# A two-layer decoder trunk: layer 0's raw weights on GpSimd's queue, transposing transfers one half product earlier, products with values and joins one later

## The chip, the cores and the metric

The kernel runs on one core of a Trainium2 chip. The metric is the device time of one execution in microseconds (us); lower is better. Five engines work side by side, each through its own instructions in order: TensorE (PE: matrix products, PEld: its weight loads), VectorE (DVE), ScalarE (ACT), GpSimd (POOL) and SyncE (SP), which here only issues transfers (DMAs). An instruction that waits holds up everything behind it on its engine. A transfer that an engine has issued is carried out by the core's 16 DMA engines, and a semaphore tells when it has landed.

## What is computed

A causal decoder trunk of two layers on 1024 rows of width 1024, all in float32. Layer 0 mixes tokens by dilated attention in three groups (g = 0, 1, 2) of eight heads of width 128, layer 1 by gated linear attention, and each is followed by a dense squared-ReLU network. Cut to the part that matters here:

```python
def dilated_attention(h, w_in, w_out):
    qkv = (h @ w_in).reshape(B, S, N_GROUPS, 3, ATTN_HEADS, HEAD_DIM)
    for g, (window, dil) in enumerate(((128, 1), (512, 4), (2048, 16))):
        q = apply_rope(qkv[:, :, g, 0], cos, sin) * HEAD_DIM ** -0.5
        k = apply_rope(qkv[:, :, g, 1], cos, sin)
        v = qkv[:, :, g, 2]
        o_g, lse_g = dilated_group_attention(q, k, v, dil, window // dil)
    alpha = softmax(stack(lses), axis=0)           # the three groups are merged
    o = sum(alpha[..., None] * stack(outs), axis=0)
    return o.reshape(B, S, ATTN_WIDTH) @ w_out
```

## The kernel before

Layer 0 has three stages. First come the values of all groups (the class `Values`), then the queries and keys of the 24 pairs of a head and a group with their attention (the class `Heads`), then the output product (`out_proj`). The change lies in the second stage, from 246 us to about 870 us of the span.

**A pair** p = 3h + g is worked off in `run_head` (L1182). The queries and keys of a pair come from seven products (slots) of 12 matrix instructions in float32r halves, and each slot is cut into two half products of six. After each of the 14 half products `advance` moves a clock by one and runs what an agenda holds for that tick, in the order of a rank. So the agenda, written by hand, sets the order of all engines' instructions: what is put at tick c + 14 comes in program order behind 14 half products of the pair that began at tick c = 14p. The pairs overlap: while the products of pair p run, the attention of pair p - 1 (`follow`) is put between them, and its last products fall into pair p + 1.

**The raw weights.** `Heads.load` (L1113) loads the weights of the next pair at tick c + 3 by four transfers of 256 KB (L1119) into two tiles named raw. ScalarE and VectorE cut them into halves (wah, wal and so on, L536 and L537) from tick c + 8 on, and the products of the next pair read these from tick c + 14 on.

**The columns.** `column` (L1122) adds up a quarter of queries or keys (c, L1127), and SP swaps the halves of its partitions for the rotary positions by two transfers (cw, L1128 and L1129). Four ticks later VectorE multiplies with cosines and sines and writes qT or kT (L1136 to L1144). The columns come at ticks 5, 11, 13 and 15.

**The attention of a pair** goes over four blocks j of 256 queries. `scores` multiplies queries and keys on TensorE (pS, L989); `soft` does the mask and the exponentials (pt, L1003 and L1005); `halves` (L1027) splits the 32-bit words into 16-bit parts on ScalarE (L1035), and GpSimd's queue writes them to DRAM (pscr, L1037); `flip` (L1040) reads them back by a transposing transfer on SP's queue (L1048); and `values` (L1059) multiplies with the values (pO, L1069), copies the result (orow, L1073) and stores it (og, L1076 to L1082). The table `POINTS` (L1191) has one row each for the ticks of scores, halves, flips and values, in that order, with one number for each j; `load_values` stands two ticks before the first scores. `SINGLE` is the table of the last two attentions, which transpose on TensorE instead. A flip waits for the write of its part to land. In group 1, and for j = 0 of group 0, a block needs two writes and two flips, else one.

**The joins.** When all three groups of a head are stored, `plan_merges` (L1300) puts the merge on the agenda: it loads half of the rows (rows, L1207, 780 KB), weighs and scales them, and joins them (om, L1231 and L1232). The halves are loaded at ticks 13 and 24 of the head's successor.

**The end of the stage.** In the last pair, the first four tiles of the output weights (`W.dma`, L136, 512 KB each) and the first half of the joined heads 0 to 3 (`ahead_h8`, name ol, L1292, 1 MB) are loaded at ticks 1 to 3, and `turned.turn(0)` transposes ol on TensorE (L260) at tick 8.

Of the kernel before, what the change touches and what calls it, by code (L numbers as in the profile page):

```python
# [20 lines left out]
P = 128  # L21
# [21 lines left out]
def hybrid_trunk(ctx, tc, x, norm_mix, norm_mlp, norm_fin, a_in, a_out, g_in, g_up, g_b, g_nw,  # L43
                 g_out, m_up, m_down, tab, msk, gmask, ident_d, out):
    nc = tc.nc
    pe, act, dve, pool, sp = nc.tensor, nc.scalar, nc.vector, nc.gpsimd, nc.sync
# [7 lines left out]
    def h8(shape, dt, name):  # L54
        return wk.tile(shape, dt, name=name, tag="h8", bufs=12)

    def k4(shape, dt, name):
        return wk.tile(shape, dt, name=name, tag="k4", bufs=25)
# [53 lines left out]
    class Weights:  # L112
# [14 lines left out]
            self.slots.append(src)  # L127
            self.by.append(by)

        def dma(self):  # L130
            n = self.ndma
            if n < len(self.slots):
                self.ndma += 1
                src = self.slots[n]
                self.raws[n] = k4([P] + list(src.shape[1:]), F32, "raw")
                sp.dma_start(self.raws[n], src)  # L136

        def prep(self, eng=dve):
            n = self.nprep
# [41 lines left out]
    W = Weights()  # L181
# [8 lines left out]
    def add_rows(w, k0, by=None):  # L190
        for k in range(2):
            W.add(w[P * (k0 + k):P * (k0 + k + 1), :], by and by(k0 + k))
# [93 lines left out]
    class Split:  # L286
# [4 lines left out]
        @staticmethod  # L291
        def at(tiles, k):
            n = 4 // len(tiles)
            return tiles[k // n][:, k % n, :]
# [206 lines left out]
    class Up:  # L501
# [10 lines left out]
        def load(self, p):  # L512
            if p < NP:
                self.raw[p] = [k4([P, 4, 256], F32, "raw") for _ in range(2)]
                for k in range(2):
                    sp.dma_start(self.raw[p][k], cols(self.w, 256 * p, 256, 4 * k, 4))
# [220 lines left out]
    oscr = drp.tile([S, D], F32, name="oscr")  # L737
# [363 lines left out]
    class Heads(Up):  # L1101
# [11 lines left out]
        def load(self, p):  # L1113
            if p < self.count:
                h, g = divmod(p, NG)
                self.raw[p] = [k4([P, 4, 256], F32, "raw") for _ in range(2)]
                for k in range(2):
                    for b in range(2):
                        sp.dma_start(self.raw[p][k][:, :, 128 * b:128 * b + 128],  # L1119
                                     self.w[:, 4 * k:4 * k + 4, 3 * g + b, HD * h:HD * h + HD])  # L1120

        def column(self, p, b, half, bank_, e):  # L1122
# [59 lines left out]
        def run_head(self, p):  # L1182
            self.plan(p)
            if p:
                self.follow(p - 1, 14 * p, self.POINTS if p < self.count - 1 else self.SINGLE)
            for s in self.SLOTS:
# [1 line left out]
                    self.product(p, s, range(2 * half, 2 * half + 2))  # L1188
                    advance()

        POINTS = (8, 8, 12, 12), (11, 12, 15, 16), (20, 20, 24, 24), (14, 15, 18, 19)  # L1191
        SINGLE = (8, 10, 12, 14), (12, 14, 16, 18), (14, 16, 18, 20)

        def follow(self, p, c, points):
# [8 lines left out]
    def merge_load(h, half):  # L1203

        rows = (h8([P, 4, NG, HD + 2], F32, "rows") if h == HEADS - 1 and half else
                r6([P, 4, NG, HD + 2], "rows"))
        sp.dma_start(rows, og[h][512 * half:512 * half + 512].rearrange("(t p) g c -> p t g c", p=P))  # L1207
        return rows

    def merge_weights(rows):  # L1210
        d = sm([P, 4, NG], "md")
        e = sm([P, 4, NG], "me")
        z = sm([P, 4], "mz")
        dve.tensor_reduce(z, rows[:, :, :, HD + 1], axis=AX.X, op=OP.min)
        dve.tensor_tensor(d, z.unsqueeze(2).to_broadcast([P, 4, NG]), rows[:, :, :, HD + 1], op=OP.subtract)
        act.activation(e, d, AF.Exp)
        return d, e, z

    def merge_shares(rows, d, e, z):
        dve.tensor_tensor(d, e, rows[:, :, :, HD], op=OP.mult)  # L1220
        dve.tensor_reduce(z, d, axis=AX.X, op=OP.add)
        dve.reciprocal(z, z)
        dve.tensor_tensor(e, e, z.unsqueeze(2).to_broadcast([P, 4, NG]), op=OP.mult)

    def merge_scale(rows, e, t):
        for g in range(NG):
            act.activation(rows[:, t, g, 0:HD], rows[:, t, g, 0:HD], AF.Copy, scale=e[:, t, g:g + 1])

    def merge_join(rows, eng):
        o = t2([P, 4, HD], F32, "om")  # L1230
        eng.tensor_tensor(o, rows[:, :, 0, 0:HD], rows[:, :, 1, 0:HD], op=OP.add)  # L1231
        eng.tensor_tensor(o, o, rows[:, :, 2, 0:HD], op=OP.add)  # L1232
        return o
# [8 lines left out]
    def merges(h, done):  # L1242

        rows, part = {}, {}

        def load(half):
            rows[half] = merge_load(h, half)

        def start(half):
            part[half] = merge_weights(rows[half])  # L1250

        def finish(half):
            done(h, half, merge(rows.pop(half), *part.pop(half)))
        return load, start, finish
# [25 lines left out]
    def merged(h, half, o):  # L1280
        if h < HEADS - 1:
            sp.dma_start(oscr[512 * half:512 * half + 512, HD * h:HD * h + HD].rearrange("(b p) c -> p b c", p=P), o)
        else:
            def last():
                t_head(h, half, o)
                reached.add((0, half))
            at(clock[0] + 7, last)

    def ahead_h8(pairs):

        t = h8([P, 4, 512], F32, "ol")
        sp.dma_start(t, oscr[512 * pairs:512 * pairs + 512, 0:512].rearrange("(b p) c -> p b c", p=P))  # L1292
        return [t[:, 0:2, :], t[:, 2:4, :]]

    def ahead_k4(p):
# [4 lines left out]
    def plan_merges(h, c):  # L1300

        rows, part = {}, {}

        def load(half):
            rows[half] = merge_load(h, half)

        def weigh(half):
            part[half] = merge_weights(rows[half])

        def join(half):  # L1310
            del part[half]
            merged(h, half, merge_join(rows.pop(half), dve))
        for half in range(2):
            t = c + 13 + 11 * half
            at(t, lambda half=half: load(half))
            if half and h == HEADS - 2:
                t += 9
            at(t + 4, lambda half=half: weigh(half), 9)
            at(t + 5, lambda half=half: merge_shares(rows[half], *part[half]), 9)
            for n in range(4):  # L1320
                at(t + 6 + n, lambda half=half, n=n: merge_scale(rows[half], part[half][1], n), 9)
            at(t + 10, lambda half=half: join(half), 9)
# [429 lines left out]
    ol = []  # L1752
    turned = Turned(ol, x[0])
    for p in range(heads.count):
        h, g = divmod(p, NG)
        if g == 1 and h:
            plan_merges(h - 1, 14 * p)
        if p == heads.count - 1:
            for k in range(0, KT, 2):
                add_rows(a_out, k)  # L1760
            c = 14 * p
            at(c + 1, lambda: (W.dma(), W.dma()), 0)
            at(c + 2, lambda: (W.dma(), W.dma()), 0)
            at(c + 3, lambda: ol.extend(ahead_h8(0)), 0)
            for t in (5, 6, 7, 8):
                at(c + t, lambda: W.prep(dve), 7)
            at(c + 8, lambda: turned.turn(0), 7)
            at(c + 9, lambda: (turned.load_x(0), turned.load_x(1)))
            at(c + 11, lambda: turned.turn(1), 7)
            at(c + 17, lambda: ol.extend(ahead_h8(1)), 9)  # L1770
        heads.run_head(p)
# [7 lines left out]
    def tail():  # L1779

        c = clock[0]
        heads.follow(heads.count - 1, c, ((6, 7, 8, 9), (9, 10, 11, 12), (11, 12, 13, 14)))
        load, start, finish = merges(HEADS - 1, merged)
        rows = {}
        advance()

        def early(half):
            t = rows[half] = h8([P, 4, 512], F32, "ol2")
            sp.dma_start(t[:, :, 0:384], oscr[512 * half:512 * half + 512, 512:896].rearrange("(b p) c -> p b c", p=P))
        at(c + 7, lambda: early(0))  # L1790
        at(c + 16, lambda: early(1))
        for i, (half, h) in enumerate(((0, 4), (0, 5), (0, 6), (1, 4), (1, 5), (1, 6))):
            at(c + (13 + 3 * i if half == 0 else 21 + i), lambda half=half, h=h: t_head(h, half, rows[half][:, :, HD * (h - 4):HD * (h - 4) + HD]))
        at(c + 15, lambda: (load(0), load(1)), 9)
        at(c + 18, lambda: start(0))
        at(c + 19, lambda: finish(0))
        at(c + 20, lambda: start(1))
        at(c + 21, lambda: finish(1))
        steps.extend([advance] * 42)
# [591 lines left out]
    ol, turn1 = [], []  # L2391
# [81 lines left out]
```

## Time and profile before

| | before |
|---|---|
| median of 3 runs | 2609.16 us (2606.06 to 2611.59) |
| the profiled execution | 2608.73 us |
| its span | 2607.0 us |
| TensorE busy | 2569.7 us (99%) |
| VectorE busy | 1865.2 us (72%) |
| ScalarE busy | 1309.1 us (50%) |
| GpSimd busy | 79.3 us (3%) |
| SP's queue of transfers | 437.29 MB, 55.3% of 16 engines' span |
| GpSimd's queue of transfers | 17.05 MB, 2.1% |

The span is what the trace covers; the execution takes 1.7 us more around it. A row of a list of waits reads: who waited, for whom, us in total, how often, the longest. A row of the timeline reads: start, us, engine, line, operation, out<-in, how many, and in brackets the idle time before it and what ended it. SPq is SP's issue of a transfer; the time beside it is that of the issue, not of the transfer. A row of one line's instructions has the shortest, median and longest duration in ns, and where it issues transfers a row has the same from issue to landing. A row of windows has, for each engine, the busy time and the number of instructions, then the granted TensorE clock, the busy share of the DMA engines and what they moved.

### The profile page before, as it was taken

What the parts mean: (1) busy time and instruction counts of PE and PEld (TensorE: products, weight loads), DVE (VectorE), ACT (ScalarE), POOL (GpSimd) and SP (SyncE); (2) the same over time, 40 slices, a digit from 0 to 9 for tenths busy, and PEclk for the clock granted to TensorE, in tenths of its full rate; (3) what the DMA queues carried; (4) which work ended last, traced back from release to release, by engine and by line L of the source; (5) the groups of instructions that cost most, each with busy time, mean ns of one, the idle gap of its engine ahead of it and who ended that gap; (6) DMA issues with size and microseconds to landing.
All of it is one profiled execution on the core that took longest, in us unless ns stands there. A gap on an engine that the chain in (4) does not pass through costs nothing.

```text
span 2607.0 us, 33382 instructions
## 1 busy us (share of the span) xinstructions
PE 2569.7 (99%) x11901; PEld 2138.2 (82%) x11901; DVE 1865.2 (72%) x3018; ACT 1309.1 (50%) x2388; POOL 79.3 (3%) x132
## 2 busy tenths in 40 slices
PE   9999999999998999999999999999999999999998
PEld 7888888888787888888888888888888888888887
DVE  7745888888887668766657487887658866656567
ACT  6423566666665446555534345654426555553334
POOL 0000111111110000000000000000000000000000
PEclk9999999999999999999999999999999999999999
DMA  5543688788888732544775453463513544396543
GB/s 182 172 143 109 171 210 213 203 208 216 207 212 219 238 121 100 191 153 154 257 268 185 145 184 106 124 213 99 183 67 127 170 150 161 126 354 205 182 149 131
DMA packets 403705, 456.73 MB, mean 175 GB/s; under 512 B 92337, under 2 KB 264753, under 8 KB 403538
## 3 DMA queue, kind: packets, MB, share of 16 engines
q1 hardware_dynamic: 397250, 437.29, 55.3%
q0 software_dynamic: 6144, 17.05, 2.1%
q8 instruction: 93, 1.52, 0.2%
q14 instruction: 74, 0.61, 0.1%
q10 hardware_dynamic: 144, 0.26, 0.0%
HBM read 279.19 MB, written 133.10 MB: 158 GB/s over the span
## 4 chain that ended last, share of the span: by engine, by line
PE 87%; DMA 5%; DVE 4%; ACT 2%; SPq 1%; issue 1%; DVEq 0%; ACTq 0%
PE pX L599 15%; PE pB L1936 13%; PE pA L1936 10%; PE pV L599 9%; PE pB L830 8%; PE pA L830 5%; PE pY L599 5%; PE pZ L599 5%; PE pd L216 3%; PE pd L214 3%; PE pd L215 3%; DMA cw<-c 2%; DMA pt<-pscr 1%; PE pS L989 1%; PE pO L1069 1%
## 5 line engine op out<-in xcount | busy, mean ns | idle before, releaser
L1936 PE MATMUL pB<-dh 128*128 128x512 f32 x512 | 199.4, 389 | 0.0
L1936 PE MATMUL pB<-dh,dl 128*128 128x512 f32 x512 | 199.2, 389 | 0.0
L1936 PE MATMUL pB<-dl,dh 128*128 128x512 f32 x512 | 199.2, 389 | 0.0
L223 DVE TENSOR_TENSOR dl<-sin,dh 128x1024 fp32r<-128x1024 f32 x112 | 136.7, 1220 | 42.1 <-ACT dh L220 41.4
L220 ACT ACTIVATE dh<-sin 128x1024 fp32r<-128x1024 f32 x112 | 117.9, 1052 | 88.6 <-PE pB L1936 34.1
L220 ACT ACTIVATE dh<-kept 128x1024 fp32r<-128x1024 f32 x64 | 67.9, 1061 | 183.4 <-DVE kept L1901 138.1
L599 PE MATMUL pV<-s4h,wd 128*128 128x512 f32 x448 | 150.9, 399 | 0.0
L1936 PE MATMUL pA<-dh 128*128 128x512 f32 x384 | 149.4, 389 | 0.0
L1936 PE MATMUL pA<-dl,dh 128*128 128x512 f32 x384 | 149.4, 389 | 0.0
L1936 PE MATMUL pA<-dh,dl 128*128 128x512 f32 x384 | 149.4, 389 | 0.0
L1005 ACT ACTIVATE pt<-pt,orow 128x128 f32<-128x128 f32 (+1 forms) x192 | 84.7, 442 | 123.7 <-DVE orow L1003 122.5
L1936 PEld LDWEIGHTS pB<-dh 128*128 128x128 f32 x512 | 96.1, 188 | 20.0
L1936 PEld LDWEIGHTS pB<-dh,dl 128*128 128x128 f32 x512 | 96.1, 188 | 19.9
L1936 PEld LDWEIGHTS pB<-dl,dh 128*128 128x128 f32 x512 | 96.1, 188 | 19.9
L537 DVE TENSOR_TENSOR wal<-raw,wah 128x512 fp32r<-128x512 f32 x112 | 76.2, 686 | 41.1 <-ACT wah L536 41.1
L1069 PE MATMUL pO<-v,pt 128*128 128x128 f32 x560 | 79.2, 284 | 23.1 <-DMA pt<-pscr 22.7
L537 DVE TENSOR_TENSOR wbl<-t,wbh 128x1024 fp32r<-128x1024 f32 x56 | 68.6, 1225 | 46.3 <-ACT wbh L536 46.2
L608 ACT ACTIVATE c<-c 128x512 f32<-128x512 f32 x64 | 40.4, 631 | 118.6 <-DVE c L636 77.6
L1037 POOL DMA_DIRECT2D pscr<-pt x124 | 77.0, 621 | 752.3 <-ACT pt L1035 742.0
L1069 PEld LDWEIGHTS pO<-v,pt 128*128 128x128 f32 x560 | 73.5, 195 | 31.3 <-DMA pt<-pscr 27.7
L599 PEld LDWEIGHTS pV<-s4h,wd 128*128 128x128 f32 x448 | 84.2, 188 | 17.8 <-DVE rb L624 0.3
L223 DVE TENSOR_TENSOR dl<-kept,dh 128x1024 fp32r<-128x1024 f32 x64 | 78.4, 1225 | 24.7 <-ACT dh L220 18.7
(398 smaller groups left out, 7444.3 us busy)
## 6 DMA issues: line engine op xcount, KB each, us to landing
sin<-acts SPq DMA_DIRECT2D x112, 512.0 KB, 3.9
raw<-in_mlp_w_up_dram SPq DMA_DIRECT2D x64, 512.0 KB, 6.2
acts<-s SPq DMA_DIRECT2D x64, 512.0 KB, 3.3
raw<-in_mlp_w_down_dram SPq DMA_DIRECT2D x64, 512.0 KB, 4.7
raw<-in_attn_w_in_dram SPq DMA_DIRECT2D x98, 256.0 KB, 4.5
cw<-c SPq DMA_DIRECT2D x192, 128.0 KB, 3.2
acts<-c SPq DMA_DIRECT2D x64, 256.0 KB, 2.1
kept<-in_mlp_w_down_dram SPq DMA_DIRECT2D x32, 512.0 KB, 5.2
```

Of the source, the lines that this page charges most:

```text
L214: pe.matmul(ps, sh, mh, start=start, stop=False)
L215: pe.matmul(ps, sh, ml, start=False, stop=False)
L216: pe.matmul(ps, sl, mh, start=False, stop=stop)
L220: act.activation(hi, src, AF.Copy)
L223: dve.tensor_tensor(lo, src, hi.bitcast(F32), op=OP.subtract)
L537: self.remain(lambda: dve.tensor_tensor(lo, src, hi.bitcast(F32), op=OP.subtract))
L599: pe.matmul(st[b], u[:, k, :], v, start=first and k + n == 0, stop=k == 3 and n == 2, skip_group_check=True)
L830: pe.matmul(self.acc[s][t], a[:, c], b[:, k, :], start=fresh and m + k + v == 0, stop=m == 1 and k == 1 and v == 2, skip_group_check=True)
L1005: act.activation(pt[:, i, :128 * n], pt[:, i, :128 * n], AF.Exp, scale=-1.0, bias=m, accum_out=self.row[:, r, HD:HD + 1])
L1037: pool.dma_start(scr[512 * P * b:][:256 * P * nb * m].rearrange("(i p c) -> p i c", i=nb, p=P), part.rearrange("p (i c) -> p i c", i=nb))
L1069: pe.matmul(po[:, 2 * (j % 2) + i, :], self.turned(j, tile_, i, s), self.v[:, k0 // 128 + s, :], start=(s == 0), stop=(s == nk - 1))
L1936: pe.matmul(self.acc[s][t], a[:, k, c], b[:, k, :], start=fresh and m + k + v == 0, stop=m == 7 and k == 1 and v == 2, skip_group_check=True)
```

## The change

Four things, all in layer 0's second stage:

- The raw weights of the heads are loaded by GpSimd's queue instead of SP's (`Heads.load`). With them go the first four tiles of the output weights and the first load of ol.
- The flips of all four blocks stand one tick earlier: 13, 14, 17, 18 instead of 14, 15, 18, 19. The writes that they wait for stay at 11, 12, 15, 16.
- The products with values stand one tick later: 21, 21, 25, 25 instead of 20, 20, 24, 24.
- The joins start one tick later, at 14 and 25 instead of 13 and 24; for the second half of head 6, whose later steps are put off in addition, these stay where they were.

```diff
-        def dma(self):
+        def dma(self, by=None):
...
-                sp.dma_start(self.raws[n], src)
+                (by or sp).dma_start(self.raws[n], src)
...
-                        sp.dma_start(self.raw[p][k][:, :, 128 * b:128 * b + 128],
+                        pool.dma_start(self.raw[p][k][:, :, 128 * b:128 * b + 128],
...
-        POINTS = (8, 8, 12, 12), (11, 12, 15, 16), (20, 20, 24, 24), (14, 15, 18, 19)
+        POINTS = (8, 8, 12, 12), (11, 12, 15, 16), (21, 21, 25, 25), (13, 14, 17, 18)
...
-    def ahead_h8(pairs):
+    def ahead_h8(pairs, by=sp):
...
-        sp.dma_start(t, oscr[512 * pairs:512 * pairs + 512, 0:512].rearrange("(b p) c -> p b c", p=P))
+        by.dma_start(t, oscr[512 * pairs:512 * pairs + 512, 0:512].rearrange("(b p) c -> p b c", p=P))
...
-            t = c + 13 + 11 * half
+            t = c + 14 + 11 * half
             at(t, lambda half=half: load(half))
             if half and h == HEADS - 2:
-                t += 9
+                t += 8
...
-            at(c + 1, lambda: (W.dma(), W.dma()), 0)
-            at(c + 2, lambda: (W.dma(), W.dma()), 0)
-            at(c + 3, lambda: ol.extend(ahead_h8(0)), 0)
+            at(c + 1, lambda: (W.dma(pool), W.dma(pool)), 0)
+            at(c + 2, lambda: (W.dma(pool), W.dma(pool)), 0)
+            at(c + 3, lambda: ol.extend(ahead_h8(0, pool)), 0)
```

(The table's third row is that of the values and its fourth that of the flips.)

What this does to the order is seen in the instruction lists, where a row with - stands only in the old order at that place and one with + only in the new. First SP's list inside a pair whose attention is of group 1 (two flips to a block; pscr_92 to pscr_94 are the DRAM buffers of blocks 0 to 2, cw are the two swaps of a column):

```order
 L1048 DMA_TRANSPOSE pt<-pscr_92 128x1x256
 L1048 DMA_TRANSPOSE pt<-pscr_92 128x2x256
-L1128 DMA cw<-c 64x512
-L1129 DMA cw<-c 64x512
 L1048 DMA_TRANSPOSE pt<-pscr_93 128x1x256
 L1048 DMA_TRANSPOSE pt<-pscr_93 128x2x256
-L1119 DMA raw<-in_attn_w_in_dram 128x4x128 x4
+L1128 DMA cw<-c 64x512
+L1129 DMA cw<-c 64x512
 L1048 DMA_TRANSPOSE pt<-pscr_94 128x1x256
 L1048 DMA_TRANSPOSE pt<-pscr_94 128x2x256
```

The swap of the column of tick 15 moved from ahead of block 1's flips to behind them, and the four raw loads are gone from between the blocks.

Next TensorE's list at the place of a pair's first products with values (the row of pO; pX<-s2 are the half products of ticks 6 and 7):

```order
 L599 MATMUL pV<-s1l,wbh 128x512
 L599 MATMUL pV<-s1h,wbl 128x512
+L599 MATMUL pX<-s2h,wbh 128x512
+L599 MATMUL pX<-s2l,wbh 128x512
+L599 MATMUL pX<-s2h,wbl 128x512
+L599 MATMUL pX<-s2h,wbh 128x512
+L599 MATMUL pX<-s2l,wbh 128x512
+L599 MATMUL pX<-s2h,wbl 128x512
 L1069 MATMUL pO<-v,pt 128x128 x6
```

Six matrix instructions, one half product, now stand ahead of the products with values.

Last GpSimd's list at the end of the stage (the raw<-in_attn_w_out rows are the output weights, pscr_96 to pscr_99 the last attention with flips):

```order
+L1119 DMA raw<-in_attn_w_in_dram 128x4x128 x4
 L1037 DMA pscr_96<-pt 128x256
 L1037 DMA pscr_96<-pt 128x512
 L1037 DMA pscr_97<-pt 128x2x512
+L136 DMA raw<-in_attn_w_out_dram 128x1024 x2
 L1037 DMA pscr_98<-pt 128x2x512
+L136 DMA raw<-in_attn_w_out_dram 128x1024 x2
 L1037 DMA pscr_99<-pt 128x2x512
+L1292 DMA ol<-oscr 128x4x512
```

The last two writes of parts now stand behind one and two megabytes of output weights on their queue.

## The prediction, made before the changed kernel ran

> **What bounds the kernel now.** I read the page's span and busy times first, then TensorE's list of waits, then windows over the stage that is changed.
>
> ```profile
> span 2607.0 us, 33382 instructions
> PE pO L1069 <- DMA pt<-pscr: 22.7, 19, 7.2
> PE pS L989 <- DVE qT L1144: 3.3, 3, 2.1
> 246.00:830.00 584.00, 566.83 (x2802) 477.67 (x2801) 487.53 (x1022) 347.71 (x882) 76.44 (x124) 1.00 0.82 203
> 830.00:850.00 20.00, 12.76 (x61) 10.91 (x60) 13.14 (x20) 11.13 (x24) 0.52 (x1) 0.83 1.16 285
> PE pO L1069 <- DMA pt<-pscr: 15.5, 18, 2.1
> PE pS L989 <- DVE qT L1144: 1.2, 2, 1.0
> ```
>
> TensorE works almost all the time; all that an edit of order can win is its idle time. The first two waits are those of the whole span, the last two those of 246 to 830 us, the loop over the pairs. There TensorE is idle 584.0 - 566.8 = 17.2 us, and 15.5 us of it are 18 waits of products with values for their flips, none over 2.1 us. The nineteenth wait, 7.2 us, lies in 830 to 850, the end of the stage, where the clock falls to 0.83 as well. So the change has some 25 us (1%) to win at most. VectorE is busy 487.5 of 584 us in the loop, close behind TensorE.
>
> **The change part by part.** One pair shows how the loop's waits come about.
>
> ```profile
> 280.56 2.72 PE pX L599 x12
> L1048 SPq DMA_TRANSPOSE pt<-pscr x124: 1130/1214/5177, 287.2 to 843.5; - x124
> DMA to landing us min/median/max: 2.2/3.5/9.7
> 696.94 2.77 SPq L1048 DMA_TRANSPOSE pt<-pscr  x2
> 699.82 0.54 SPq L1128 DMA_DIRECT2D cw<-c  x1
> 700.41 0.58 SPq L1129 DMA_DIRECT2D cw<-c  x1
> 701.10 2.52 SPq L1048 DMA_TRANSPOSE pt<-pscr  x2
> 703.71 2.18 SPq L1119 DMA_DIRECT2D raw<-in_attn_w_in_dram  x4
> 705.99 2.45 SPq L1048 DMA_TRANSPOSE pt<-pscr  x2
> 708.53 0.55 SPq L1128 DMA_DIRECT2D cw<-c  x1
> 709.82 2.52 SPq L1048 DMA_TRANSPOSE pt<-pscr  x2
> 705.16 0.71 PE L1069 MATMUL pO<-v,pt 128*128 128x128 f32 x4 [1.04 <-DMA pt<-pscr]
> 713.86 0.71 PE L1069 MATMUL pO<-v,pt 128*128 128x128 f32 x4 [0.30 <-DMA pt<-pscr]
> ```
>
> The second row is one line's issues (a flip costs SP 1.2 us), the third their time to landing. SP issues without a pause from 696.94 on. Block 1's flips go out at 701.10 behind the swap of a column; block 3's at 709.82 behind four raw loads (2.18 us) and another swap. TensorE waits 1.04 us for block 1 and 0.30 for block 3.
>
> *Flips earlier.* Block 1's flips go ahead of the swap, so 701.10 - 699.82 = 1.3 us sooner; block 0's stay, since SP issues the same ahead of them, but for the rows of a merge in one pair of three (780 KB, 0.54 us of issue at 825.70, a row further down), which now go behind two blocks' flips or behind a swap; I count that at nothing, as a gain for the flips and a loss for the swap of tick 15. Blocks 2 and 3 also lose the raw loads ahead: 2.2 us, and block 3 another 1.1 us of swap.
>
> *Values later.* Twelve products take 2.72 us, so a half product ahead of the values is 1.36 us of useful work. Together block 1 gains 1.3 + 1.36 = 2.7 us, blocks 2 and 3 from 3.6 us on. The longest wait of the loop is 2.1 us: by this sum all 15.5 us go. I keep 3 us for landings that come late because the raw loads now run beside them (below), and count **12.5 us** won. What is behind the values (orow, og, the joins) moves one tick with them; the merge has its own ticks moved too, and nobody on TensorE waits for it, so I count it at nothing. That cover ends at head 7's joins, which are not in this table.
>
> *The swap behind the flips.* This is what I fear most.
>
> ```profile
> DMA to landing us min/median/max: 2.2/3.2/6.4
> 706.19 0.67 DVE L1136 TENSOR_TENSOR cw<-cw,tab 128x512 f32<-128x512 f32 x1
> 707.50 1.18 DVE L1144 TENSOR_TENSOR qT<-c,cw 128x512 f32<-128x512 f32 x1
> 708.74 1.16 PE L989 MATMUL pS<-kT,qT 128*128 128x128 f32 x8
> DVE cw L1136 <- DMA cw<-c: 30.1, 28, 3.3
> ```
>
> The first row is the swaps' time to landing, the last VectorE's waits for them in the loop. The swap issued at 700.41 lands by the median at 703.6; VectorE takes it at 706.19, and qT is done at 708.68, 0.06 us before the scores that read it. So the swap has 2.6 us to spare, and the scores behind it none. The flips put it off by 1.2 us in groups 0 and 2, and by 2.5 us in group 1. That fits, barely; behind it on SP stand the next flips, and for it waits VectorE, with 30.1 us of such waits already. Bounds: nothing, or 2.5 us for each of 22 attentions (55 us) if VectorE had no slack. Nearest is the row with 2.6 us to spare, so I take about 0.2 us for each, **4.5 us** lost, most of it where TensorE, no longer waiting for values, comes to its scores sooner than VectorE's qT.
>
> *Raw loads on GpSimd.*
>
> ```profile
> L1037 POOL DMA_DIRECT2D pscr<-pt x124: 538/555/738, 282.6 to 829.8; - x124
> DMA to landing us min/median/max: 1.8/3.1/9.6
> 699.22 1.17 POOL L1037 DMA_DIRECT2D pscr<-pt  x2 [0.18 <-issue]
> 717.42 0.72 POOL L1037 DMA_DIRECT2D pscr<-pt  x1 [17.03 <-ACT pt L1035]
> DMA to landing us min/median/max: 3.2/4.5/5.8
> 707.54 0.63 ACT L536 ACTIVATE wah<-raw 128x512 fp32r<-128x512 f32 x1
> ```
>
> The trace has no raw load on this queue. The first two rows are the writes' issues there and their time to landing: the issues take 0.55 us for 128 rows and 0.73 for 256 (738 is the longest), so 512 rows come to about 0.73 + 2 x 0.18 = 1.1 us, an estimate from these; four take 4.4 us. GpSimd is idle from 700.4 to 717.4, so they hide there and hold up no write. They may go out from 700.4, not 703.71; with the 4.5 us of the fifth row, the median to landing of the raw loads on SP's queue, they land before ScalarE takes them at 707.54 (the last row). Bounds: nothing, or, if a load took as long as a write at its worst (9.6 us from 700.4), 2.5 us late at ScalarE for each pair. I take nothing, since the write's median of 3.1 us is nearest. But their megabyte now shares the DMA engines with block 1's flips and the swap, instead of standing ahead of block 2's: that is the 3 us kept above.
>
> [...] The row first: 124 writes were issued between 282.6 and 829.8 us, with VectorE busy over four fifths of the time, and none took over 0.74 us. [...]
>
> *The end of the stage.*
>
> ```profile
> 825.70 0.54 SPq L1207 DMA_DIRECT2D rows<-og  x1
> 828.89 1.06 SPq L136 DMA_DIRECT2D raw<-in_attn_w_out_dram  x2
> 831.35 3.98 SPq L1048 DMA_TRANSPOSE pt<-pscr  x1
> 836.51 0.38 SPq L1292 DMA_DIRECT2D ol<-oscr  x1
> 829.81 0.71 POOL L1037 DMA_DIRECT2D pscr<-pt  x1 [0.75 <-ACT pt L1035]
> DMA to landing us min/median/max: 7.5/8.4/9.2
> 846.64 1.04 PE L260 MATMUL pT<-ident,ol 128*128 128x128 f32 x8
> 842.00:844.00 2.00, 2.00 (x7) 1.65 (x7) 1.41 (x2) 1.43 (x2) 0.00 (x0) 0.50 1.01 382
> ```
>
> Block 1's flip at 831.35 stands behind 1 MB of output weights, hence the 7.2 us. Now it goes before them, and that wait goes. But ol, issued at 836.51, lands about 8.4 us later (the median of its two loads), at 845, and TensorE transposes it at 846.64, two ticks behind. All of this is bandwidth: the DMA engines are at 1.16 in 830 to 850. Unless ol lands sooner, TensorE only waits at another place; and block 3's write (829.81) now stands behind 2 MB. Bounds: nothing, or 7.2 + 2 us for the clock of 0.50 that followed the pause (the last row: four microseconds at half speed). I take **2 us**, nearer to nothing, since ol's landing is the nearest row.
>
> The clock also fell behind one of the loop's waits:
>
> ```profile
> 396.00:400.00 4.00, 3.24 (x12) 2.60 (x11) 3.97 (x6) 4.00 (x13) 0.00 (x0) 0.65 0.86 228
> ```
>
> At 0.65 for 4 us that cost 1.4 us; I count **1 us** of it as won.
>
> Sum: 12.5 - 4.5 + 2 + 1 = 11 us. The profiled execution took 2608.73 us (span 2607.0), 0.4 below the median of the runs: 2608.7 - 11 = **2598 us**.
>
> **The rivals.** *Two: the wait only moves.* Flips that land no sooner, since their writes land late or the raw loads share the engines, and scores that wait for qT in their place. For it speaks the 0.06 us at 708.74. It would keep three quarters of the 15.5 us: 4 us won, nothing at the end, 2605. *Three: everything is won*, 15.5 + 1 in the loop and 7 at the end: 2585. Against it speaks VectorE, busy 487.5 of 584 us. *Four, slower: GpSimd's issue is held up.* If each of four issues waited for one of VectorE's operations, some 1.2 us as the 1.18 above, the last load would land 5 us later; ScalarE would wait at its cut with the exponentials queued behind. It decides from 2.4 us late on, since the loads can go 3.3 us sooner than before. At 1 us for each of 23 pairs, less what is won: 2608.7 + 23 - 11 = 2621. *Five, slower: the swap becomes the bound.* If flips and raw loads together put it off by over 2.6 us, VectorE and then the scores wait in every pair: at 1.5 us, 22 x 1.5 = 33 us, against 15.5 won, 2626.
>
> **How the numbers follow.** The forecast holds 0.48 (2590 to 2603), rival two 0.22, three 0.13, four 0.06, five 0.11. A measurement of this kernel can tell about 0.2%, 5.2 us, from no change: faster is below 2604, the forecast and three entirely and a quarter of two, 0.66; no change the rest of two, 0.17; slower are four and five, 0.17. The range runs from three's 2585 to 2613, and leaves four and five out.
>
> **What would show it.** Right, if TensorE's waits for pt<-pscr fall from 15.5 us in the loop to about 3, those for qT grow to some 5, and issues of raw on GpSimd take about 1.1 us. Two shows as waits for qT above 8 us; four as issues of raw far over 1.1 us and ScalarE waiting for raw; five as VectorE's waits for cw well above 30.1 us. At the end, a transposition of ol that waits says the pause was only moved. I am wrong altogether if time appears outside the stage.

## The result, and the profile after

| | before | after |
|---|---|---|
| median of 4 runs each | 2607.61 us | 2721.4 us |
| smallest and largest | 2605.8 to 2611.59 | 2719.16 to 2726.83 |
| span of the profiled execution | 2607.0 us | 2718.0 us |
| TensorE busy | 2569.7 us | 2609.7 us |
| ScalarE busy | 1309.1 us | 1311.1 us |
| SP's queue of transfers | 437.29 MB | 408.97 MB |
| GpSimd's queue of transfers | 17.05 MB | 45.37 MB |

The changed kernel is slower: 1.0437 times the time before (95% interval 1.0416 to 1.0459), 114 us. The forecast was 11 us faster, and its range ended at 2613 us. Of all executions of all runs one, of the kernel with the flips alone, took 4343.28 us at a granted clock of 0.556 and is left out (with it that median would be 2651.55 us, which later expectations quote).

First TensorE's list of waits over the whole span of the changed kernel (us in total, times, the longest).

```profile
PE pX L599 <- ACT e L1164: 50.2, 20, 4.1
PE pS L989 <- DVE qT L1144: 39.8, 15, 5.6
PE pO L1069 <- DMA pt<-pscr: 6.2, 4, 3.6
```

Then the window over the stage (busy times of TensorE, its weight loads, VectorE, ScalarE and GpSimd, then clock and share of the DMA engines):

```profile
246.00:930.00 684.00, 602.39 (x2794) 499.65 (x2794) 483.08 (x1011) 345.31 (x872) 143.64 (x213) 0.94 0.70 170
```

The wait that the change aims at is nearly gone, 6.2 us where 22.7 stood. In its place TensorE waits 50.2 us for ScalarE to clear a bank (e, a copy of a column's first part) and 39.8 us for qT. The span grew by 111 us. TensorE's idle time, span less busy time, grew from 37.3 to 108.3, that is by 71. The other 40 us are busy time for the same number of matrix instructions (11901 in both): the granted clock fell, to 0.94 in the stage. Before, the same window reads thus:

```profile
246.00:930.00 684.00, 657.47 (x3274) 555.04 (x3273) 553.48 (x1153) 389.13 (x987) 76.95 (x124) 0.99 0.80 204
```

The DMA engines were less busy afterwards (0.70 against 0.80 on average over the window), which speaks against bandwidth as what ran out. Next the other engines' waits in this window:

```profile
POOL raw L1119 <- issue: 185.3, 57, 7.0
DVE t L565 <- DMA raw<-in_attn_w_in_dram: 86.9, 21, 5.9
ACT wah L536 <- DMA raw<-in_attn_w_in_dram: 86.5, 21, 6.9
DVE cw L1136 <- DMA cw<-c: 37.4, 26, 3.3
DVE mz L1214 <- DMA rows<-og: 25.6, 11, 4.0
```

And the raw loads' line with its issues (ns, shortest, median, longest), and their time to landing:

```profile
L1119 POOL DMA_DIRECT2D raw<-in_attn_w_in_dram x96: 747/756/883, 219.4 to 922.0; - x96
DMA to landing us min/median/max: 3.1/4.1/7.9
```

ScalarE and VectorE now wait some 87 us each for the raw weights; before, ScalarE's waits of this kind were 0.2 us. Yet a single issue takes 0.76 us, and a single load lands after 4.1 us, no later than on SP's queue (4.5). What is long is the pause between the issues. One pair in the timelines of GpSimd, ScalarE, VectorE and TensorE shows where it leads; the last two rows are the time to landing of the first and the third of the four loads:

```profile
601.37 0.77 POOL L1119 DMA_DIRECT2D raw<-in_attn_w_in_dram  x1 [0.25 <-issue]
605.81 0.76 POOL L1119 DMA_DIRECT2D raw<-in_attn_w_in_dram  x1 [3.67 <-DVE c L1137]
610.28 0.76 POOL L1119 DMA_DIRECT2D raw<-in_attn_w_in_dram  x1 [3.71 <-issue]
616.62 0.75 POOL L1119 DMA_DIRECT2D raw<-in_attn_w_in_dram  x1 [5.58 <-issue]
616.34 0.63 ACT L536 ACTIVATE wah<-raw 128x512 fp32r<-128x512 f32 x1 [6.89 <-DMA raw<-in_attn_w_in_dram]
620.12 0.69 DVE L565 TENSOR_TENSOR t<-raw,t 128x512 f32<-128x512 f32 x1 [5.53 <-DMA raw<-in_attn_w_in_dram]
630.80 0.50 PE L599 MATMUL pX<-s2h,wbh 128*128 128x512 f32 x1 [4.03 <-ACT e L1164]
DMA to landing us min/median/max: 4.1/4.1/4.1
DMA to landing us min/median/max: 6.0/6.0/6.0
```

Four loads that took 2.2 us to issue on SP's queue are spread over 16 us here. ScalarE stands 6.89 us at its cut, until the third has landed, with the exponentials and the copies e queued behind it; VectorE stands 5.53 us until the fourth has; and later on TensorE waits 4.03 us for a copy e. This last step is in part argued: right before that copy, at 630.15, ScalarE stands 2.69 us with no cause named. VectorE, late since 620.12, has just ended a column (kT, at 630.07), and e, c and cw share the eight buffers of `t2`, so e most likely waited for one of that column's.

Between the issues the timeline shows nothing: the releaser named at 605.81 (VectorE's c) has nothing to do with a load of weights, and two of the others have none at all. But the landings fit. The first load lands 4.1 us after 601.37, at 605.4, and the second goes out at 605.81; the third lands 6.0 us after 610.28, at 616.3, and the fourth goes out at 616.62. Each load goes out 0.3 to 0.4 us after the one before it has landed.

### The profile page after: what moved, and what is told of

It is laid out like the page before. It is cut to its first block, busy times and chain, and to the rows that moved or that the text cites. A ratio compares the mean times of both kernels' runs of the same rounds, so it can differ in the third digit from the quotient of the medians.

```text
span 2718.0 us, 33465 instructions
## 1 busy us (share of the span) xinstructions
PE 2609.7 (96%) x11901; PEld 2162.3 (80%) x11901; DVE 1865.1 (69%) x3018; ACT 1311.1 (48%) x2388; POOL 155.1 (6%) x233
## 3 DMA queue, kind: packets, MB, share of 16 engines
q1 hardware_dynamic: 345458, 408.97, 48.9%
q0 software_dynamic: 14672, 45.37, 6.5%
## 4 chain that ended last, share of the span: by engine, by line
PE 80%; DMA 7%; DVE 5%; issue 5%; ACT 2%; SPq 1%; POOL 0%; DVEq 0%; POOLq 0%; ACTq 0%
PE pX L599 13%; PE pB L1936 12%; PE pA L1936 10%; PE pV L599 9%; PE pB L830 6%; PE pA L830 5%; PE pZ L599 4%; PE pY L599 4%; PE pd L216 3%; PE pd L214 3%; PE pd L215 3%; DMA rows<-og 2%; PE pS L989 2%; DMA cw<-c 2%; DMA raw<-in_attn_w_in_dram 2%
## 5 line engine op out<-in xcount | busy, mean ns | idle before, releaser
L599 PE MATMUL pV<-s4h,wd 128*128 128x512 f32 x448 | 159.0, 418 | 2.0 <-ACT e L1164 2.0
L599 PE MATMUL pX<-s2h,wbh 128*128 128x512 f32 x224 | 96.8, 432 | 49.2 <-ACT e L1164 49.1
L989 PE MATMUL pS<-kT,qT 128*128 128x128 f32 (+1 forms) x384 | 77.9, 345 | 39.8 <-DVE qT L1144 39.8
L536 ACT ACTIVATE wah<-raw 128x512 fp32r<-128x512 f32 x112 | 68.8, 623 | 86.5 <-DMA raw<-in_attn_w_in_dram 86.5
L599 PEld LDWEIGHTS pV<-s4h,wd 128*128 128x128 f32 x448 | 89.8, 200 | 25.1 <-ACT e L1164 5.5
L1119 POOL DMA_DIRECT2D raw<-in_attn_w_in_dram x96 | 72.9, 759 | 542.7 <-DVE dl L815 218.1
L989 PEld LDWEIGHTS pS<-kT,qT 128*128 128x128 f32 x384 | 62.4, 201 | 51.2 <-DVE qT L1144 41.6
L565 DVE TENSOR_TENSOR t<-raw,t 128x512 f32<-128x512 f32 x56 | 38.8, 692 | 88.1 <-DMA raw<-in_attn_w_in_dram 86.9
```

The lines of the kernel that those rows point to most:

```text
L599: pe.matmul(st[b], u[:, k, :], v, start=first and k + n == 0, stop=k == 3 and n == 2, skip_group_check=True)
L989: pe.matmul(ps[:, i, :128 * n], self.qT[:, 128 * b:128 * b + 128], self.kT[:, k0:k0 + 128 * n], start=True, stop=True)
L1119: pool.dma_start(self.raw[p][k][:, :, 128 * b:128 * b + 128], self.w[:, 4 * k:4 * k + 4, 3 * g + b, HD * h:HD * h + HD])
```

## The experiments

All times are compared with the kernel before, run beside them on the same chip; where parts are set against each other, the ratio is turned into us of a kernel of 2607 us.

**The two halves.** The first run is the change without its moves to GpSimd's queue, the second the kernel before with `Heads.load` alone on that queue, the third the changed kernel with one setting of the build raised from 1024 to 1728.

```diff
-                        pool.dma_start(self.raw[p][k][:, :, 128 * b:128 * b + 128],
+                        sp.dma_start(self.raw[p][k][:, :, 128 * b:128 * b + 128],
...
-            at(c + 1, lambda: (W.dma(pool), W.dma(pool)), 0)
+            at(c + 1, lambda: (W.dma(), W.dma()), 0)
...
```

> The changed kernel with all transfers back on SP's queue: flips one tick earlier, values and joins one later. Theory Q (the loss is in GpSimd's queue, which takes a raw load of 512 rows only when the one before it has landed): 2590 to 2606 us, waits of products with values for flips in the loop down from 15.5 to about 3 us, no waits for raw. Theory T (the moved ticks cost the time: swaps and joins late, scores waiting for qT): 2690 us or more, with some 40 us of scores waiting for qT.

```diff
-                        sp.dma_start(self.raw[p][k][:, :, 128 * b:128 * b + 128],
+                        pool.dma_start(self.raw[p][k][:, :, 128 * b:128 * b + 128],
```

> The kernel before with the heads' raw loads alone on GpSimd's queue, all ticks as before. Theory Q: 2690 to 2730 us, raw loads issued some 4.5 us apart, ScalarE's cut wah waiting over 60 us for raw. Theory T: within 1% of 2608 us.

```diff
-    nc = _bacc.Bacc("TRN2", target_bir_lowering=False, num_devices=1, dynamic_dma_scratch_size=1024)
+    nc = _bacc.Bacc("TRN2", target_bir_lowering=False, num_devices=1, dynamic_dma_scratch_size=1728)
```

> [...] Theory L (VectorE holds up GpSimd's issue): 2721 us within 0.3%, the loads 4.5 us apart as before.

Measured: the ticks alone 2661.11 us, 1.0208 (1.0188 to 1.0228); the raw loads alone 2665.11, 1.0232 (1.0203 to 1.0261); the raised setting 2672.75, 1.0262 (1.0233 to 1.029). So there are two losses, 54 and 60 us, and they add up to the 114 of the change; each theory had foreseen only one of them. The raised setting alone takes 46 us off it. Waits of GpSimd, ScalarE and TensorE in the run with the raw loads alone, then GpSimd's timeline and ScalarE's waits with the raised setting:

```profile
POOL raw L1119 <- issue: 202.4, 62, 9.3
ACT wah L536 <- DMA raw<-in_attn_w_in_dram: 90.4, 26, 7.3
PE pO L1069 <- DMA pt<-pscr: 55.5, 39, 6.0
```

```profile
577.02 1.51 POOL L1119 DMA_DIRECT2D raw<-in_attn_w_in_dram  x2 [0.17 <-issue]
579.96 0.75 POOL L1119 DMA_DIRECT2D raw<-in_attn_w_in_dram  x1 [1.43 <-issue]
581.76 0.76 POOL L1119 DMA_DIRECT2D raw<-in_attn_w_in_dram  x1 [1.05 <-issue]
```

```profile
ACT wah L536 <- DMA raw<-in_attn_w_in_dram: 4.3, 6, 1.0
```

With 1728 the four loads go out within 5.5 us instead of 16, and ScalarE's waits for them fall from 86.5 to 4.3 us, with the same line, the same queue and the same work on VectorE. So these waits hang on the setting; how it acts on the queue was not shown. Two things were not as theory Q had it. The third load, which was to follow the second within 1.2 us, came after a pause of 1.43 us; what it waited for was not shown. And the time, expected at 2600 to 2650 us, stayed at 2672.75, since the ticks cost 54 us of their own. Of the 68 us left, 14 are not the ticks'; these were not taken apart.

With the raw loads alone the loss shows at TensorE as waits for flips, 55.5 us against 22.7 before. The parts that ScalarE splits come late behind its cut, and their writes stand behind the loads on GpSimd's queue; how much each of these costs was not measured.

**How many go out in a row.** The kernel before, with 18 transfers to DRAM that nothing reads put on GpSimd's queue in layer 1, where it is otherwise idle: six each of 512, 256 and 128 rows, all of 256 KB (the edit shows the first six).

```diff
+    for n in range(6):
+        to = drp.tile([P, 4, 128], F32, name=f"probe512_{n}")
+        pool.dma_start(to, wsrc[:, 0:4, 128 * n:128 * n + 128])
...
```

> The kernel before with 18 transfers added on GpSimd's queue in layer 1, behind the two fills of gc, where nothing on GpSimd is waited for: six of 512 rows, six of 256 and six of 128 rows, from weights to DRAM tiles that nobody reads. [...] Theory L: all back to back, 0.6 to 0.8 us apart, or held up as VectorE is busy, whatever their rows.

Measured: 2605.55 us in one execution, and in GpSimd's timeline, of which these are five rows (L2119 are the 512 rows, L2122 the 256, L2125 the 128):

```profile
977.08 0.74 POOL L2119 DMA_DIRECT2D probe<-in_attn_w_in_dram  x1 [0.32 <-issue]
980.71 0.71 POOL L2119 DMA_DIRECT2D probe<-in_attn_w_in_dram  x1 [2.88 <-issue]
1001.50 2.01 POOL L2122 DMA_DIRECT2D probe<-in_attn_w_in_dram  x3 [4.24 <-issue]
1009.27 1.72 POOL L2125 DMA_DIRECT2D probe<-in_attn_w_in_dram  x3
1012.28 1.58 POOL L2125 DMA_DIRECT2D probe<-in_attn_w_in_dram  x3 [1.29 <-issue]
```

The six issues of 512 rows stand apart, each 2.88 to 3.38 us after the one before it ended; of 256 rows three go out in a row from 1001.50 on, and of 128 rows three, then three more after a pause of 1.29 us. The issue itself takes about 0.7 us for 512 as for 256 rows (0.70 to 0.74 and 0.65 to 0.78), and 0.55 for 128 (1.72 and 1.58 for three). The bytes are the same in all 18 transfers, so they alone do not set how many go out in a row here; what does was not shown.

**The parts of the ticks.** Each is the kernel before with one piece. First the table of ticks with the rows of the merge left at their old ticks, and then each kind of move alone.

```diff
-        POINTS = (8, 8, 12, 12), (11, 12, 15, 16), (20, 20, 24, 24), (14, 15, 18, 19)
+        POINTS = (8, 8, 12, 12), (11, 12, 15, 16), (21, 21, 25, 25), (13, 14, 17, 18)
```

> The kernel before with the new table of ticks alone: flips one half product sooner, values one later; the joins' rows stay at their old ticks 13 and 24, and the raw weights stay on SP's queue. Theory R (the ticks cost their 55 us because the rows of a merge, 780 KB, now stand on SP's queue right ahead of a swap, which then lands some 7 us late): 2590 to 2606 us, TensorE's waits for qT below 12 us. Theory S (rival five of the prediction: the swap is late because it stands behind two blocks' flips, whatever the rows do): 2640 us or more, waits for qT of 40 us or more.

```diff
-            t = c + 13 + 11 * half
+            t = c + 14 + 11 * half
...
-                t += 9
+                t += 8
```

> The kernel before with the joins alone one tick later (rows at ticks 14 and 25); flips, values and raw weights as before. At tick 25 the rows now come right ahead of the swap of tick 13 of the next pair's columns less two flips' head start, at tick 14 right ahead of block 0's flips and the swap of tick 15. Theory R: 2635 to 2665 us, with TensorE's waits for qT of 30 us or more. Theory S: within 0.5% of 2606 us.

```diff
+        POINTS = (8, 8, 12, 12), (11, 12, 15, 16), (20, 20, 24, 24), (13, 14, 17, 18)
```

> The kernel before with the flips alone one half product sooner (13, 14, 17, 18); values, joins and raw weights as before. Theory R: 2596 to 2612 us, since the rows keep their place ahead of flips. Theory S: 2640 us or more, TensorE's waits for qT of 40 us or more and VectorE's waits for cw above 60 us.

```diff
+        POINTS = (8, 8, 12, 12), (11, 12, 15, 16), (21, 21, 25, 25), (14, 15, 18, 19)
```

> The kernel before with the values alone one half product later (21, 21, 25, 25). Theories R and S: 2595 to 2606 us, up to 10 us of TensorE's waits for the flips go and no other wait grows. Rival V (the later values hold the buffers of pt, orow and og longer and put off the stores that the merge needs): 2615 us or more.

| | median us | ratio | interval | us |
|---|---|---|---|---|
| table of ticks, rows kept | 2648.05 | 1.0158 | 1.0142 to 1.0173 | +41 |
| joins alone | 2615.33 | 1.0028 | 1.0018 to 1.0039 | +7 |
| flips alone | 2649.74 | 1.0164 | 1.0146 to 1.0182 | +43 |
| values alone | 2603.13 | 0.9984 | 0.9974 to 0.9993 | -4 |

My own theory R, that the rows of the merge carry the loss, failed: the joins alone cost 7 us, and the flips alone, with the rows at their tick, 43. Singly the pieces make 43 + 7 - 4 = 46 of the 54 us; the other 8 come only with the pieces together and were not taken apart. But theory S did not simply win. In the run with the flips alone, TensorE's waits in the stage are for the flips themselves, and three kinds of transfer are late at once:

```profile
PE pO L1069 <- DMA pt<-pscr: 37.8, 13, 6.5
DVE cw L1136 <- DMA cw<-c: 77.1, 31, 5.1
ACT wah L536 <- DMA raw<-in_attn_w_in_dram: 28.3, 23, 2.8
DVE mz L1214 <- DMA rows<-og: 14.9, 11, 2.8
```

SP's timeline at one of the places, and TensorE's behind it; the last two rows are SP's timeline of the kernel before at the corresponding place of a pair:

```profile
615.26 0.54 SPq L1207 DMA_DIRECT2D rows<-og  x1
615.91 1.46 SPq L1048 DMA_TRANSPOSE pt<-pscr  x1
623.13 2.08 PE L1069 MATMUL pO<-v,pt 128*128 128x128 f32 x8 [4.58 <-DMA pt<-pscr]
590.36 0.54 SPq L1207 DMA_DIRECT2D rows<-og  x1
591.00 2.50 SPq L1048 DMA_TRANSPOSE pt<-pscr  x2
```

The flips' tick moves nothing but SP's list (a flip is issued there and nowhere else; the other engines' lists are the same in both traces). So the 43 us are the price of what now stands behind a flip, which waits for its write: swaps, rows, raw loads. The timelines show the rows of the merge. Before, they went ahead of the flips of block 0; now block 0's flips stand ahead, the 780 KB go out between the blocks, and TensorE can start on the flip of block 1, issued right behind them at 615.91, only 7.2 us later, after a wait of 4.58 us.

**Which of the three.** With the table of ticks, the first half's rows one tick sooner:

> As the run with the new table of ticks and the rows at their old ticks, but the first half's rows one tick sooner (12), so that they stand ahead of all flips on SP's queue again, as before the change; raw weights on SP's queue. Theory R2 (the flips themselves are not dear; they hold the queue until their writes have landed, the 780 KB of rows behind them go out late and stand right ahead of the next flips and the swap of tick 15): 2595 to 2617 us, TensorE's waits for the flips below 12 us. Theory S (the swap is late because it stands behind flips that wait for their writes, rows or no rows): 2635 us or more, VectorE's waits for cw still above 60 us.

Measured 2645.12 us, 1.0144 (1.0127 to 1.016). It did not decide, since the rows at tick 12 waited themselves for the results they read (SP stands 21.0 us at them, in 7 waits), and the swaps behind them were later still (VectorE's waits for cw 90.6 us). The next runs start from the flips alone. The swaps of the queries' columns go to GpSimd's queue, with a control that does only this to the kernel before:

```diff
-            sp.dma_start(w[0:64, :], c[64:128, :])
-            sp.dma_start(w[64:128, :], c[0:64, :])
+            by = sp if b else pool
+            by.dma_start(w[0:64, :], c[64:128, :])
+            by.dma_start(w[64:128, :], c[0:64, :])
```

> As the run with the flips alone one half product sooner (2651.6 us), but the swaps of the queries' columns (those of ticks 5 and 15, which the sooner flips put behind a second block's flips) go to GpSimd's queue, where no flip stands. Theory S (the loss is the swap waiting on SP's queue behind flips that wait for their writes): nearly all of the 44 us come back but for what GpSimd's queue costs by itself: the run with the swaps alone moved, plus or minus 8 us; VectorE's waits for cw back below 45 us. Theory F (sooner flips cost by themselves, for instance by the rows of a merge that they hold up): 2635 us or more.

> The control: the kernel before with only the swaps of the queries' columns on GpSimd's queue. A swap there may stand behind a write whose part is not ready yet. Theories S and F both: 2600 to 2620 us.

Then the raw loads put ahead of block 2's flips again, the rows ahead of block 0's, and both:

```diff
-            at(c + 3, lambda: self.load(p + 1))
+            at(c + 2, lambda: self.load(p + 1))
```

> The flips alone one half product sooner (2651.6 us by itself), with the raw loads one half product sooner too, so that they stand ahead of block 2's flips on SP's queue again. Since the flips' ticks move nothing but SP's list, their 44 us must come from what they stand ahead of there: the swaps of the queries' columns, the rows of a merge, the raw loads. If the raw loads carry a third or more: 2637 us or less, ScalarE's waits for raw back below 10 us. If they carry next to nothing: 2645 to 2655 us.

```diff
-            at(t, lambda half=half: load(half))
+            at(t, lambda half=half: load(half), 5 if half else 2)
```

> The flips alone one half product sooner, with the first half's rows of a merge put ahead of block 0's flips on SP's queue again, at their old place behind the swap of tick 13. If the rows carry a third or more of the 44 us (the 4.6 us wait of products with values in one pair of three): 2637 us or less. If they carry next to nothing: 2645 to 2655 us.

> Both of these edits with the sooner flips: against the kernel before, SP's list now differs only by the swaps of the queries' columns (ticks 5 and 15), which stand behind one block's flips more. So its loss is the price of the swap alone, rival five of the prediction: by the rival 2622 to 2630 us, by the prediction's own step (0.2 us for each of 22) 2595 to 2608 us.

| flips sooner, and | median us | ratio | interval | us |
|---|---|---|---|---|
| nothing else | 2649.74 | 1.0164 | 1.0146 to 1.0182 | +43 |
| raw loads ahead again | 2643.33 | 1.0133 | 1.0114 to 1.0152 | +35 |
| rows ahead again | 2636.51 | 1.0112 | 1.0096 to 1.0127 | +29 |
| both ahead again | 2625.15 | 1.0063 | 1.0048 to 1.0078 | +16 |
| swaps on GpSimd's queue | 2639.0 | 1.012 | 1.0105 to 1.0135 | +31 |
| control: the swaps alone moved | 2599.82 | 0.997 | 0.9957 to 0.9983 | -8 |

Putting the raw loads ahead gives back 8 us, the rows 14, both 26; the remaining 16 are the swaps behind one block's flips more, which is all that SP's list still differs in. The parts are not independent: taking the swaps away first gives back only 4 us against its control; TensorE then waits 33.0 us for flips and ScalarE 40.6 us for raw weights. In the run with both ahead, the waits in the stage are:

```profile
PE pO L1069 <- DMA pt<-pscr: 24.7, 24, 2.7
DVE cw L1136 <- DMA cw<-c: 80.4, 35, 5.2
ACT wah L536 <- DMA raw<-in_attn_w_in_dram: 7.1, 7, 1.5
DVE mz L1214 <- DMA rows<-og: 3.4, 7, 0.9
```

The waits for raw and for rows have gone back, those for the swap have not. And even here the flips that were put sooner win nothing: TensorE's waits for them are 24.7 us against 22.7 before.

In the change itself the rows stand at tick 14, behind two blocks' flips and right ahead of the swap of tick 15. The run of the ticks alone shows what that does, in SP's, VectorE's and TensorE's timelines:

```profile
622.07 3.86 SPq L1048 DMA_TRANSPOSE pt<-pscr  x3
626.03 0.53 SPq L1207 DMA_DIRECT2D rows<-og  x1
626.66 0.62 SPq L1128 DMA_DIRECT2D cw<-c  x1
DMA to landing us min/median/max: 7.2/7.2/7.2
633.30 0.17 DVE L1214 TENSOR_REDUCE mz<-rows 128x4 f32<-128x12 f32 x1 [2.69 <-DMA rows<-og]
635.52 1.06 DVE L1144 TENSOR_TENSOR qT<-c,cw 128x512 f32<-128x512 f32 x1
636.63 1.35 PE L989 MATMUL pS<-kT,qT 128*128 128x256 f32 x6 [3.81 <-DVE qT L1144]
```

The swap issued at 626.66 lands 7.2 us later (the fourth row is this one swap's), VectorE stands 2.69 us at the merge's first instruction until the rows are there, and qT comes 3.81 us late at the scores. The two causes lie close together: the swap has landed at 633.9, and VectorE, after the merge's instruction, comes to it at 634.21, so either alone would have held qT up nearly as long. VectorE's waits for rows are 28.4 us in that run, against 3.6 before, and TensorE's waits for qT 48.2.

**The end of the stage**, and the values together with it:

```diff
-            at(c + 1, lambda: (W.dma(), W.dma()), 0)
-            at(c + 2, lambda: (W.dma(), W.dma()), 0)
-            at(c + 3, lambda: ol.extend(ahead_h8(0)), 0)
+            at(c + 1, lambda: (W.dma(pool), W.dma(pool)), 0)
+            at(c + 2, lambda: (W.dma(pool), W.dma(pool)), 0)
+            at(c + 3, lambda: ol.extend(ahead_h8(0, pool)), 0)
...
```

> The kernel before with only the end of the stage changed: the first four tiles of the output weights and the first load of ol go to GpSimd's queue. By the sums so far (ticks +54 us, raw weights +59, change +114) it is worth 0 to 3 us: 2603 to 2611 us. By the prediction's step on the end of the stage: 2605, 2 us won. [...]

> The kernel before with the values one half product later, and the end of the stage on GpSimd's queue. If the two add up with the run of the end alone: that run's difference from before, less 4.7 us. A version that beats both kernels would have 2603 us or less.

Measured: the end alone 2616.3 us, 1.0032 (1.0022 to 1.0042), 8 us lost; with the later values 2609.65, 1.0007 (0.9998 to 1.0015). GpSimd's timeline of the first with the time to landing of its last two writes (issued at 827.99 and 830.76), and TensorE's waits from 800 to 900 us:

```profile
828.70 1.23 POOL L136 DMA_DIRECT2D raw<-in_attn_w_out_dram  x2
830.76 0.72 POOL L1037 DMA_DIRECT2D pscr<-pt  x1 [0.83 <-ACT e L1164]
845.83 0.81 POOL L1292 DMA_DIRECT2D ol<-oscr  x1 [14.34 <-issue]
DMA to landing us min/median/max: 14.2/15.7/17.2
```

```profile
PE pO L1069 <- DMA pt<-pscr: 14.2, 3, 8.2
```

The waits for the last flips doubled from 7.2 to 14.2 us, since the last writes stand behind the output weights and land only after 14.2 and 17.2 us, with SP standing at their flips; and ol was issued 15 us after the write ahead of it.

**A faster version.** The control above, the swaps of the queries' columns on GpSimd's queue and nothing else, is the fastest kernel here: 0.997 of the time before. In its stage TensorE's waits are:

```profile
PE pO L1069 <- DMA pt<-pscr: 10.5, 14, 3.4
PE pS L989 <- DVE qT L1145: 3.8, 7, 0.9
```

Those for the flips fall from 22.7 us to 10.5, with no swap left ahead of them on SP's list but those of the keys, and those for qT hardly grow. With the later values too it was no better:

> Values one half product later (2603.1 us alone) and the swaps of the queries' columns on GpSimd's queue. Were the 7.8 us of TensorE's waits for qT that the later values leave due to swaps behind flips, 2595 to 2600 us; otherwise the sum of both single runs.

Measured 2603.31 us, 0.9985 (0.9975 to 0.9994): the sum of the two was not reached. TensorE still waits 8.0 us for flips and 8.7 us for qT there, so swaps behind flips were not what held qT up with the later values.

## Why the prediction was wrong, step by step

**The bound was read rightly, the win from it was too large.** TensorE's waits for the flips did go. But the step "by this sum all 15.5 us go", with 12.5 counted, added the gains of two moves. The later values alone bring 4 us, and not by less idle time: this only moves, since waits for e (10.7 us) and for qT (7.8) appear in that run. TensorE's idle time there is 36.7 us, against 37.3 before; what fell is its busy time, by 4.3 us. The sooner flips brought nothing by themselves, even with only the swaps behind them. The sum asked how much sooner SP can issue a flip, and not whether its write has landed by then, which keeps SP standing at the flip.

**"I count that at nothing"**, said of the rows that now stand behind flips or ahead of the swap, is the first step that failed, and so is the merge's "nobody on TensorE waits for it, so I count it at nothing". TensorE doesn't wait for the merge itself. But VectorE does, with the column of qT behind it in its list, and so does all that stands behind the 780 KB on SP's queue. It cost 14 us where the rows fell between two blocks' flips; where they stand right ahead of the swap, both together made 3.8 us in the pair shown. The joins by themselves cost 7 us.

**The swap behind the flips** was named as what I feared most, and mis-sized: 4.5 us by the row with 2.6 us to spare, 16 measured. The term put only the flips' issue (1.2 and 2.5 us) in front of the swap, and not SP's wait for the write that the flip reads. With the flips alone sooner, SP's waits at flips add up to 122 us, against 101 before, and those put down to the write itself to 24.0, against 10.3. That the run which leaves the swaps alone behind the flips took 2625 us and rival five said 2626 is chance: the rival's price was 33 us, less 15.5 us won, and here the price was 16 with nothing won. The rival had the right place and twice the size. In the change itself VectorE's waits for cw are only 37.4 us (78.2 with the ticks alone); there it stands 86.9 us for raw weights instead.

**The raw loads on GpSimd** are the largest error: "I take nothing" where 60 us were lost. The estimate of the issue was even too high (1.1 us; 0.76 measured). What failed is "four take 4.4 us": it took for granted that the next load can be issued while the one before is under way. The bound above was wrong for the same reason: it let one load be as late as the worst write, 2.5 us at ScalarE, where four loads behind one another made it 6.89. No row of before showed two transfers of 512 rows in flight on this queue, and the range should have held the case that they follow each other.

**Rival four** had the right place and the wrong cause. ScalarE did wait for raw, but an issue never took over 0.883 us, and with the setting at 1728 ScalarE's waits for raw fell to 4.3 us beside the same work on VectorE. So VectorE is not what holds the loads up here; that it would was the rival's supposition, and no run shows it. The rival's price, 1 us for each pair, was also below the 2.6 (60 us in 23 pairs) that were measured.

**The end of the stage**: 2 us won were forecast, 8 were lost when it was changed alone. The prediction noted that block 3's write would stand behind 2 MB, and took the value nearer to nothing all the same. What share of the 114 us is the end's cannot be told: the ticks and the raw loads already make up the whole sum, and in the changed kernel the waits there are different ones.

**The clock**: 1 us was counted as won. Instead 40 of the 111 us are matrix instructions at a lower clock. It goes with the waits in most runs: the clock in the stage is 0.96 with the ticks alone and 0.95 with the raw loads alone, against 0.99 before, and 1.00 with the swaps alone moved. But the sum of the waits does not settle it. With the joins alone TensorE's idle time is 36.9 us, no more than the 37.3 before, and yet the clock is 0.98 and the busy time 5.8 us longer, which is all of that run's loss. What makes the clock fall, beyond this, stays open.

## What to carry to other kernels

Here SP's list of transfers behaved like an engine's: the flips alone one tick sooner cost 43 us, by what stands behind them. So before an item that waits is put sooner, list what stands behind it there, each with its slack, and count the item's wait (up to 3.0 us for a write in that run) and not only its issue (1.2 us for a flip). Before loads are moved to another queue, look for how many of that size the queue holds in flight; GpSimd idle and the DMA engines at 0.80 in the stage of the kernel before did not answer that, and the raw loads, moved alone, cost 60 us. And a transfer of several hundred KB belongs where nothing urgent stands behind it, whoever needs its data: the 780 KB between two blocks' flips cost 14 us.

## What was new of the hardware

With the setting at 1024, GpSimd's queue took the raw loads of 512 rows one at a time in the pair shown: the next goes out 0.3 to 0.4 us after the one before has landed. The pause until then is 3.7 to 5.6 us in that pair, and 2.88 to 3.38 us lie between the issues of 512 rows in the probe; the trace shows it as idle time with no cause or with a chance releaser. Three of 256 rows went out in a row (2.01 us in all), and with the setting at 1728 the four raw loads went out within 5.5 us instead of 16. Issues take about 0.7 us for 256 rows as for 512. And pauses of TensorE were not the whole loss: of 111 us, 71 were pauses and 40 busy time at a lower clock (0.94 in the stage, 0.99 before).
